# Hybrid decoder block: constant fills moved to VectorE, input buffers moved to the other end of SBUF, small parameter loads and compression weights requested by ScalarE

## The chip, the cores and the metric

The kernel runs on one core of a Trainium2 chip. The metric is the device time of one execution in microseconds (us). The kernel before took 747.08 us, the median of three runs between 744.39 and 748.1 us. A kernel has five engines here: PE (TensorE, matrix products), DVE (VectorE), ACT (ScalarE), POOL (GpSimd) and SP (SyncE), which in this kernel only requests transfers (DMAs).

## What is computed

One layer of a decoder for 512 tokens of width 1024: RMSNorm of `x`, one wide input projection, three token mixers side by side, their gated merge, an output projection, an embedding added through a gate, and a final RMSNorm. Cut to what the start of the kernel does:

```python
h = _rmsnorm(x, norm_g[i])                  # 512 x 1024
proj = h @ w_in[i]                          # every mixer reads columns of this
nkc, nvc = ...                              # 2 x 128 columns of proj
blk = kv[:, idx] + pe[:, None, :]           # _compress: windows of 32 tokens, step 16
hid = silu(einsum('bnlgd,ldh->bngh', blk, w1))
k_cmp, v_cmp = einsum('bngh,hd->bngd', hid, w2)
r, k, v, wl, al = split(xs + (prev - xs) * mu)   # RWKV-7 mixer, columns of proj
```

## The kernel before

Everything that PE multiplies is split into a high part in a short float format and the rest ("high" and "low"), so each product is three matmuls. Weights of the projections come in pieces of 512 columns per partition: SP requests a piece `wr` (L76), ACT rounds it to its high part `wh` (L78), and VectorE or GpSimd forms the rest `wl` (L79). There are four buffers `wr`, so a fifth piece is requested when the first `wl` is done. Two pieces make one block of 128 output columns.

The start of the program goes as follows. GpSimd fills and masks small constant tiles (`trib`, `cmask`, `smask`, `hind`, `hm` and others). SP requests the four 512 KB tiles of `x` into `xs_`, then the first four pieces `wr`, then 14 small transfers of parameters into the tile `prow` (L267: ten parameter vectors and four pieces of `cmp_pe`). For each tile t of `x`, in this order: ACT squares it and sums the squares (`sqj`, L214), VectorE finishes the mean (`rsx`, L215), GpSimd takes the power -0.5 (L216), VectorE scales the tile (L217), PE transposes it in two halves (`xt_ps`, L222), VectorE multiplies each half by the norm's gain (`tg`, L224), ACT rounds it to `hH` (L225, eight of them, kept in the list `hcp`), and GpSimd (first half) or VectorE (second half) forms `hL` (L226).

Then come the two projections `kc` and `vc` that the compression needs, each in two halves of 256 tokens: four groups of 24 matmuls, each evacuated from PSUM by four ACT copies into `kc2` (L264, L265), which stand behind the last `hH` by a written order (`issue_after(hcp[-1])`). PSUM has two buffers `mm_ps` for such groups. After them PE begins block 12 of the RWKV columns (24 matmuls 128x512, then block 4 and so on). Between them stands the compression: 64 small matmuls `hid` that need `w1t`, the compression's weights (L291, four transfers of 512 KB), and `blk`, which is `kc2` plus `pe`. `w2t` (L286, four transfers of 32 KB) is needed later.

The order on each engine is not written by hand. A scheduler at build time orders the instructions, and each engine runs its own list in that order. It also gives each requested transfer one of eight counters, DMAHW0 to DMAHW7, in turn over all queues. A request waits until the transfer that had its counter before has landed.

SBUF pools are stacked from two ends. Pools without a side start at the left; a pool opened after another one has closed takes the same addresses, and its first writers wait for the last readers of the old one. The pool `xp` holds the tiles of `x` and all of `sqj` and `tg`; the pool `cpp`, opened later on the left, holds `kc2`, `w2t`, `w1t` and `blk`.

Of the kernel before, what the change touches and what calls it, by code (L numbers as in the profile page):

```python
# [45 lines left out]
def hybrid_kernel(ctx, tc, x, p, norm_g, w_in, cmp_w1, cmp_w2, cmp_pe, sg_ln_g, sg_ln_b, sg_w, sg_b,  # L46
# [3 lines left out]
    V, S, G, PE, SY = nc.vector, nc.scalar, nc.gpsimd, nc.tensor, nc.sync  # L50
# [45 lines left out]
    identb = const.tile([128, 128], BF, name="identb")  # L96
    V.tensor_copy(identb, ident)
    trib = const.tile([128, 128], BF, name="trib")
    G.memset(trib, 0.0)
    G.affine_select(out=trib, in_=trib, pattern=[[-1, 128]], compare_op=OP.is_ge, fill=NEG, base=0,  # L100
                    channel_multiplier=1)
    cmask = const.tile([128, 4, 32], BF, name="cmask")
    G.memset(cmask, 0.0)
    G.affine_select(out=cmask, in_=cmask, pattern=[[128, 4], [-16, 32]], compare_op=OP.is_ge, fill=NEG,
                    base=-31, channel_multiplier=1)
    rowm = const.tile([128, 1], F32, name="rowm")
    G.memset(rowm, 1.0)
    G.affine_select(out=rowm, in_=rowm, pattern=[[0, 1]], compare_op=OP.is_ge, fill=0.0, base=-31,
                    channel_multiplier=1)
    gmask = const.tile([128, 2, 64], BF, name="gmask")  # L110
    G.memset(gmask, 1.0)
    for r in (0, 64):
        for ar in range(2):
            G.affine_select(out=gmask[r:r + 64, ar, :], in_=gmask[r:r + 64, ar, :], pattern=[[1, 64]],
                            compare_op=OP.is_ge, fill=0.0, base=ar - 1, channel_multiplier=-1)
    smask = const.tile([128, 8, 64], BF, name="smask")
    G.memset(smask, 1.0)
    G.memset(smask[:, :, 0:1], 0.0)
    tri = const.tile([128, 128], BF, name="tri")
    G.memset(tri, 1.0)  # L120
    G.affine_select(out=tri, in_=tri, pattern=[[1, 128]], compare_op=OP.is_ge, fill=0.0, base=0,
                    channel_multiplier=-1)
    mhalf = const.tile([128, 32], F32, name="mhalf")
    G.memset(mhalf, -0.5)
    bones = const.tile([128, 128], BF, name="bones")
    G.memset(bones, 0.0)
    G.memset(bones[0:64, 0:64], 1.0)
    G.memset(bones[64:128, 64:128], 1.0)
    hind = const.tile([128, 4, 8], F32, name="hind")
    G.memset(hind, 0.0)  # L130
    for q in range(4):
        for e in range(2):
            G.memset(hind[e * 64:e * 64 + 64, q, 2 * q + e:2 * q + e + 1], 1.0)

    ng8 = const.tile([8, 128], F32, name="ng8")
    ngp = const.tile([128, 8], F32, name="ngp")
# [4 lines left out]
    def pc(nm, i=0, n=1):  # L141
        return par[:, pcol[nm] + i:pcol[nm] + i + n]
# [28 lines left out]


    hcp = []
    xp_ctx = ExitStack()
    xp = xp_ctx.enter_context(tc.tile_pool(name="xp", bufs=1))
    xps = xp_ctx.enter_context(tc.tile_pool(name="xps", bufs=XP, space=PSUM))
    xs_ = xp.tile([128, 4, 1024], F32, name="xs_")
    ssx = xp.tile([128, 4], F32, name="ssx")
# [1 line left out]
    S.dma_start(ng8, norm_g[0].rearrange("(a b) -> a b", b=128))  # L180
    for t in range(4):
        SY.dma_start(xs_[:, t, :], x[t * 128:(t + 1) * 128, :])
    pw_ctx = ExitStack()
    pw = pw_ctx.enter_context(tc.tile_pool(name="pw", bufs=1, side="right"))
    prow = pw.tile([128, 128], F32, name="prow")
    G.memset(prow, 0.0)
    row = 0
    pls = []
    for nm, src in (("mu", rk_mu), ("w0", rk_w0), ("a0", rk_a0),
# [11 lines left out]
                        cmp_pe[0, kv, lh * 16:lh * 16 + 16, :]))  # L201
    row += 32
    assert row <= 128

    dr = {}
    for nm, w in (("su", 512), ("sv", 512), ("sz", 512), ("rz", 512), ("nz", 512), ("y1", 512), ("sg", 512)):
# [31 lines left out]
    kcst = const.tile([128, 2, 2, 32], R, name="kcst")  # L238
    vcst = const.tile([128, 2, 128], R, name="vcst")
    hm = const.tile([128, 4], F32, name="hm")  # L240
    G.memset(hm, 0.0)
    for hh in range(4):
        G.memset(hm[32 * hh:32 * hh + 32, hh:hh + 1], 1.0)
    cp_ctx = ExitStack()
    cpp = cp_ctx.enter_context(tc.tile_pool(name="cpp", bufs=1))
    cps = cp_ctx.enter_context(tc.tile_pool(name="cps", bufs=1, space=PSUM))
# [5 lines left out]
    for half in range(2):  # L252
        c0 = half * 256
        for kv in range(2):
# [7 lines left out]
            with tc.issue_after(hcp[-1]):  # L262
                for g in range(2):
                    S.copy(kc2[0:64, kv, g, c0:c0 + 256], ps[g * 64:g * 64 + 64, :256])  # L264
                    S.copy(kc2[64:128, kv, g, c0 - sh:c0 + 240], ps[g * 64:g * 64 + 64, 16 - sh:256])  # L265
    for o, i in pls:
        SY.dma_start(o, i)  # L267
    pp_ps = cps.tile([128, 128], F32, tag="par", name="par_ps")
    PE.transpose(pp_ps, prow, ident)
    V.tensor_copy(par, pp_ps)  # L270
# [12 lines left out]
    w2t = cpp.tile([128, 2, 128], F32, name="w2t")  # L283
    for kv in range(2):
        for d in range(2):
            SY.dma_start(w2t[:, kv, d * 64:d * 64 + 64], cmp_w2[0, kv])  # L286
    w1, bl = [], []
    for kv in range(2):
        w1t = cpp.tile([128, 16, 128], F32, tag="w1t", name="w1t", bufs=2)
        for lh in range(2):  # L290
            SY.dma_start(w1t[lh * 64:lh * 64 + 64], cmp_w1[0, kv, lh * 16:lh * 16 + 16].rearrange("l d h -> d l h"))  # L291
        blk = cpp.tile([128, 16, 64], F32, tag="blk", name="blk", bufs=2)
        src = kc2[:, kv].rearrange("p g (n l) -> p l (g n)", l=16)
        V.tensor_tensor(blk, src, pc("pe", kv * 16, 16).unsqueeze(2).to_broadcast([128, 16, 64]), OP.add)
        w1.append(w1t)
        bl.append(blk)
# [68 lines left out]
    for i, src in ((0, rk_w2), (1, rk_a2)):  # L365
        a, o = (slice(0, 64), slice(64, 128)) if i == 0 else (slice(64, 128), slice(0, 64))
# [447 lines left out]
    for i in ATT:  # L814
# [21 lines left out]
        for g in range(2):  # L836
# [13 lines left out]
            for b in range(2):  # L850
# [3 lines left out]
                for hh in range(4):  # L854
                    h = g * 4 + hh
# [167 lines left out]
```

## Time and profile before

| | us |
|---|---|
| median of 3 runs | 747.08 (744.39 to 748.1) |
| the profiled execution, its own time | 744.63 |
| its span in the profile | 742.8 |
| PE busy in the span | 714.5 (96%) |
| ScalarE, VectorE, GpSimd busy | 353.8, 408.6, 287.0 |

The span is what the profile covers, from the first to the last instruction; 1.8 us of the execution lie around it. PE is busy almost throughout, so a delay matters where PE stands still, and a gain elsewhere matters only if it lets PE start sooner.

### The profile page before, as it was taken

To read this page: it belongs to the slowest core of one execution; us is meant where nothing else is said; L and a number is where in the kernel's file an instruction comes from. 1 tells how busy PE (TensorE), PEld (TensorE's weight loads), DVE (VectorE), ACT (ScalarE), POOL (GpSimd) and SP (SyncE) were. 2 spreads that over 40 slices of the span, in tenths; PEclk is the share of its full clock that TensorE was granted. 3 is DMA by queue.
4 is the path that set the end of the run, shared out by engine and by line. 5 is a ranking of instruction groups with operands and counts; after the bars stand their busy time and mean duration, and the time that the engine had idled before them with its cause. 6 is when DMAs were issued, how large, how long until landed. Compare 5 with 4: busy or idle time off the path is not lost.

```text
span 742.8 us, 13074 instructions
## 1 busy us (share of the span) xinstructions
PE 714.5 (96%) x4941; PEld 606.7 (82%) x4941; DVE 408.6 (55%) x776; ACT 353.8 (48%) x743; POOL 287.0 (39%) x275
## 2 busy tenths in 40 slices
PE   4999999999999999989999999989999999999995
PEld 4888788999878987779877778867877888998995
DVE  6531587758843863565676565397555223226345
ACT  6554555542363342335565554576554333227453
POOL 6444640120220263300144345333445565356563
PEclk9999999999999999999999999999999999999999
DMA  5853122125536364427433212201228334132212
GB/s 194 188 140 100 48 81 71 41 85 146 156 105 224 101 184 117 116 86 232 124 97 103 58 43 71 71 16 42 53 62 268 96 91 127 59 114 72 80 63 114
DMA packets 106689, 78.73 MB, mean 106 GB/s; under 512 B 5569, under 2 KB 97282, under 8 KB 106626
## 3 DMA queue, kind: packets, MB, share of 16 engines
q1 hardware_dynamic: 105890, 75.27, 35.5%
q10 hardware_dynamic: 736, 2.63, 0.9%
q8 instruction: 39, 0.64, 0.4%
q14 instruction: 24, 0.20, 0.1%
HBM read 67.91 MB, written 9.96 MB: 105 GB/s over the span
## 4 chain that ended last, share of the span: by engine, by line
PE 88%; DVE 4%; ACT 2%; DMA 2%; issue 1%; POOL 1%; SPq 1%; ACTq 0%; POOLq 0%; DVEq 0%
PE mm_ps L62 70%; PE s_ps L62 3%; PE o_ps L62 2%; PE g_ps L62 2%; PE p_ps L875 2%; DMA w1t<-in_cmp_w_dram 1%; PE Yp L62 1%; DVE mx L861 1%; PE u_ps L62 1%; ACT wh L78 1%; PE xt_ps L222 1%; PE r_ps L62 1%; PE mx_ps L62 1%; DVE pl L879 1%; PE bk_ps L477 1%
## 5 line engine op out<-in xcount | busy, mean ns | idle before, releaser
L79 POOL TENSOR_TENSOR wl<-wr,wh 128x512 fp32r<-128x512 f32 x144 | 192.6, 1346 | 278.9 <-ACT wh L78 257.6
L78 ACT CAST wh<-wr 128x512 fp32r<-128x512 f32 (+1 forms) x194 | 119.4, 620 | 166.5 <-PE mm_ps L62 114.9
L62 PE MATMUL mm_ps<-hH,wh 128*128 128x512 f32 (+1 forms) x440 | 174.9, 398 | 3.3 <-ACT wh L78 1.9
L62 PE MATMUL mm_ps<-hL,wh 128*128 128x512 f32 (+1 forms) x440 | 171.6, 390 | 0.0
L62 PE MATMUL mm_ps<-hH,wl 128*128 128x512 f32 (+1 forms) x440 | 171.1, 389 | 0.0
L62 PEld LDWEIGHTS mm_ps<-hH,wh 128*128 128x128 f32 x440 | 83.5, 190 | 20.7 <-ACT wh L78 2.2
L62 PEld LDWEIGHTS mm_ps<-hH,wl 128*128 128x128 f32 x440 | 83.2, 189 | 17.4 <-issue 0.2
L62 PEld LDWEIGHTS mm_ps<-hL,wh 128*128 128x128 f32 x440 | 83.6, 190 | 16.5 <-issue 0.2
L62 PE MATMUL mm_ps<-wh,hL 128*128 128x256 f32 (+1 forms) x224 | 65.0, 291 | 0.0
L62 PE MATMUL mm_ps<-wh,hH 128*128 128x256 f32 (+1 forms) x224 | 63.8, 286 | 0.0
L62 PE MATMUL mm_ps<-wl,hH 128*128 128x256 f32 (+1 forms) x224 | 63.7, 285 | 0.0
L79 DVE TENSOR_TENSOR wl<-wr,wh 128x512 fp32r<-128x512 f32 (+1 forms) x50 | 38.0, 768 | 26.8 <-ACT wh L78 26.7
L62 PEld LDWEIGHTS mm_ps<-wh,hL 128*128 128x128 f32 x224 | 42.2, 188 | 1.1 <-issue 0.5
L62 PEld LDWEIGHTS mm_ps<-wh,hH 128*128 128x128 f32 x224 | 42.1, 188 | 1.2 <-issue 0.5
L62 PEld LDWEIGHTS mm_ps<-wl,hH 128*128 128x128 f32 x224 | 42.2, 188 | 0.5
L879 DVE TENSOR_TENSOR pl<-p_ps,ph 128x512 fp32r<-128x512 f32 x40 | 27.1, 685 | 25.7 <-ACT ph L878 25.6
L62 PE MATMUL mm_ps<-ysH,wh 128*128 128x512 f32 x96 | 38.6, 402 | 0.1
L62 PE MATMUL mm_ps<-ysL,wh 128*128 128x512 f32 x96 | 38.4, 400 | 0.2 <-DVE ysL L725 0.2
L62 PE MATMUL mm_ps<-ysH,wl 128*128 128x512 f32 x96 | 38.2, 398 | 0.0
L862 ACT ACTIVATE P<-s_ps,mx 128x512 f32<-128x512 f32 (+3 forms) x64 | 33.4, 531 | 7.9 <-DVE mx L861 5.5
L62 PE MATMUL mm_ps<-wh,mH 128*128 128x256 f32 x128 | 35.9, 286 | 0.0
L62 PE MATMUL mm_ps<-wl,hT 128*128 128x256 f32 x128 | 35.8, 281 | 0.0
(337 smaller groups left out, 1434.6 us busy)
## 6 DMA issues: line engine op xcount, KB each, us to landing
wr<-in_w_in_dram SPq DMA_DIRECT2D x130, 256.0 KB
wr<-in_w_branch_dram SPq DMA_DIRECT2D x24, 256.0 KB
wr<-in_w_o_dram SPq DMA_DIRECT2D x16, 256.0 KB
wr<-in_w_ple_gate_dram SPq DMA_DIRECT2D x16, 256.0 KB
xs__129<-in_x_dram SPq DMA_DIRECT2D x4, 512.0 KB
w1t<-in_cmp_w_dram SPq DMA_DIRECT2D x4, 512.0 KB
x<-in_x_dram ACTq DMA_DIRECT2D x4, 512.0 KB
out_dram<-x SPq DMA_DIRECT2D x8, 256.0 KB
```

What stands on the lines that cost most here:

```text
L62: return PE.matmul(o, a, b, start=start, stop=stop, **kw).ins
L78: S.copy(h[:, :m], raw[:, :m])
L79: ph_["l"].tensor_tensor(l[:, :m], raw[:, :m], f(h[:, :m]), OP.subtract)
L222: PE.transpose(ps[:, k, :], xs_[:, t, (4 * a + k) * 128:(4 * a + k + 1) * 128], ident)
L477: PE.transpose(ps[:, c - c0, :], bk[:, c, 0:2].rearrange("p s t -> p (s t)"), ident)
L861: V.tensor_reduce(mx[:, hh:hh + 1], s_ps[:, :W], axis=AX.X, op=OP.max, negate=True)
L862: S.activation(P[:, hh, :W], s_ps[:, :W], AF.Exp, bias=mx[:, hh:hh + 1], accum_out=sm[:, hh:hh + 1])
L875: PE.transpose(p_ps[:, hh * 128:hh * 128 + 128], P[:, hh, kt * 128:kt * 128 + 128], ident)
L879: V.tensor_tensor(pl, p_ps, f(ph), OP.subtract)
```

## The change

It has four parts. Most fills of constant tiles go from GpSimd to VectorE, and so does the fill of `prow`; the masks themselves (`affine_select`) stay on GpSimd. The pools `pw` and `xp` are opened on the right, so `xp` no longer shares addresses with `cpp`. The 14 parameter loads into `prow` are requested by ScalarE (`S.dma_start`), in the code just behind the requests for `x`. The eight requests for `w2t` and `w1t` go from SP to ScalarE, each behind the last `hH` (`hcp[-1]`).

```diff
-    G.memset(trib, 0.0)
+    V.memset(trib, 0.0)
     G.affine_select(out=trib, in_=trib, pattern=[[-1, 128]], compare_op=OP.is_ge, fill=NEG, base=0,
                     channel_multiplier=1)
...
-    G.memset(hind, 0.0)
+    V.memset(hind, 0.0)
     for q in range(4):
         for e in range(2):
-            G.memset(hind[e * 64:e * 64 + 64, q, 2 * q + e:2 * q + e + 1], 1.0)
+            V.memset(hind[e * 64:e * 64 + 64, q, 2 * q + e:2 * q + e + 1], 1.0)
...
     hcp = []
+    pw_ctx = ExitStack()
+    pw = pw_ctx.enter_context(tc.tile_pool(name="pw", bufs=1, side="right"))
     xp_ctx = ExitStack()
-    xp = xp_ctx.enter_context(tc.tile_pool(name="xp", bufs=1))
+    xp = xp_ctx.enter_context(tc.tile_pool(name="xp", bufs=1, side="right"))
...
     for t in range(4):
         SY.dma_start(xs_[:, t, :], x[t * 128:(t + 1) * 128, :])
-    pw_ctx = ExitStack()
-    pw = pw_ctx.enter_context(tc.tile_pool(name="pw", bufs=1, side="right"))
     prow = pw.tile([128, 128], F32, name="prow")
-    G.memset(prow, 0.0)
+    V.memset(prow, 0.0)
...
     assert row <= 128
+    for o, i in pls:
+        S.dma_start(o, i)
...
-    for o, i in pls:
-        SY.dma_start(o, i)
     pp_ps = cps.tile([128, 128], F32, tag="par", name="par_ps")
...
     for kv in range(2):
         for d in range(2):
-            SY.dma_start(w2t[:, kv, d * 64:d * 64 + 64], cmp_w2[0, kv])
+            with tc.issue_after(hcp[-1]):
+                S.dma_start(w2t[:, kv, d * 64:d * 64 + 64], cmp_w2[0, kv])
...
         for lh in range(2):
-            SY.dma_start(w1t[lh * 64:lh * 64 + 64], cmp_w1[0, kv, lh * 16:lh * 16 + 16].rearrange("l d h -> d l h"))
+            with tc.issue_after(hcp[-1]):
+                S.dma_start(w1t[lh * 64:lh * 64 + 64],
+                            cmp_w1[0, kv, lh * 16:lh * 16 + 16].rearrange("l d h -> d l h"))
```

The built programs show where the requests came to stand. First ScalarE's list at the start of the program, before (all of its first rows up to the first rounding of `x`):

```order
L180 DMA ng_115<-in_norm_g_dram 8x128
L214 ACT_TABLE_LOAD
L214 ACTIVATE sqj,ssx<-xs__129 128x1024 [waits DMAHW1_49]
L214 ACTIVATE sqj,ssx<-xs__129 128x1024 [waits DMAHW2_49]
L214 ACTIVATE sqj,ssx<-xs__129 128x1024 [waits DMAHW3_49,Activation_49]
L214 ACTIVATE sqj,ssx<-xs__129 128x1024 [waits DMAHW4_49,Activation_49]
L225 CAST hH<-tg 128x4x128 [waits DVE_49] x4
```

And in the changed program, from the eighth row of the list; ahead of these stand the requests for `norm_g` and six of the parameters:

```order
L205 DMA prow<-in_rk_lnx_g_dram 4x128 [waits DMAHW7_49]
L205 DMA prow<-in_rk_lnx_b_dram 4x128 [waits DMAHW0_49]
L205 DMA prow<-in_ple_norm_g_dram 8x128 [waits DMAHW1_49]
L205 DMA prow<-in_sg_b_dram 8x128 [waits DMAHW2_49]
L205 DMA prow<-in_cmp_pe_dram 16x64 [waits DMAHW3_49]
L205 DMA prow<-in_cmp_pe_dram 16x64 [waits DMAHW4_49]
L205 DMA prow<-in_cmp_pe_dram 16x64 [waits DMAHW5_49]
L205 DMA prow<-in_cmp_pe_dram 16x64 [waits DMAHW6_49]
L216 ACT_TABLE_LOAD
L216 ACTIVATE sqj,ssx<-xs__132 128x1024 x2
L216 ACTIVATE sqj,ssx<-xs__132 128x1024 [waits Activation_49] x2
```

All 14 requests moved ahead of the table load and of the first square, and the squares have no wait of their own on a transfer any more.

SP's list at the start, before:

```order
L182 DMA xs__129<-in_x_dram 128x1024 x4
L76 DMA wr<-in_w_in_dram 128x4x128 x3
L76 DMA wr<-in_w_in_dram 128x4x128 [waits DMAHW0_49]
L267 DMA prow<-in_rk_mu_dram 13x128 [waits DMAHW1_49,Pool_49]
L267 DMA prow<-in_rk_w_dram 4x128 [waits DMAHW2_49]
```

And in the changed program, from the same place:

```order
L184 DMA xs__132<-in_x_dram 128x1024 x4
L76 DMA wr<-in_w_in_dram 128x4x128
L76 DMA wr<-in_w_in_dram 128x4x128 [waits DMAHW1_49]
L76 DMA wr<-in_w_in_dram 128x4x128 [waits DMAHW3_49]
L76 DMA wr<-in_w_in_dram 128x4x128 [waits DMAHW5_49]
L76 DMA wr<-in_w_in_dram 128x4x128 [waits DMAHW7_49,DVE_49]
```

The parameters are gone from SP's list. With 14 transfers now taking counters in between, the four tiles of `x` have DMAHW1, 2, 3 and 5, and the first four pieces `wr` have DMAHW7, 1, 3 and 5. So the second, third and fourth piece wait for the first, third and fourth tile of `x`; and on ScalarE `lnx_g` waits for the first piece, `ple_norm_g` for the second, the first part of `cmp_pe` for the third and its third part for the fourth.

The third place is ScalarE's list behind the last `hH`, before:

```order
L225 CAST hH<-tg 128x4x128 [waits DVE_49]
L264 COPY kc_267<-mm_ps 64x256 [waits DVE_49,PE_49,Pool_49]
L265 COPY kc_267<-mm_ps 64x240
L264 COPY kc_267<-mm_ps 64x256
L265 COPY kc_267<-mm_ps 64x240
L264 COPY kc_267<-mm_ps 64x256 [waits PE_49]
L265 COPY kc_267<-mm_ps 64x240
L264 COPY kc_267<-mm_ps 64x256
L265 COPY kc_267<-mm_ps 64x240
L78 CAST wh<-wr 128x512 [waits DMAHW4_49,PE_49]
L78 CAST wh<-wr 128x512 [waits DMAHW5_49,PE_49]
```

And in the changed program, behind the last `hH` and the first two copies:

```order
L266 COPY kc_281<-mm_ps 64x256
L267 COPY kc_281<-mm_ps 64x240
L287 DMA w2t<-in_cmp_w_dram 128x64 [waits DMAHW3_49]
L287 DMA w2t<-in_cmp_w_dram 128x64 [waits DMAHW4_49]
L287 DMA w2t<-in_cmp_w_dram 128x64 [waits DMAHW5_49]
L287 DMA w2t<-in_cmp_w_dram 128x64
L266 COPY kc_281<-mm_ps 64x256 [waits PE_49]
L267 COPY kc_281<-mm_ps 64x240
L266 COPY kc_281<-mm_ps 64x256
L267 COPY kc_281<-mm_ps 64x240
L293 DMA w1t<-in_cmp_w_dram 64x16x128 [waits DMAHW1_49]
L293 DMA w1t<-in_cmp_w_dram 64x16x128 [waits DMAHW3_49]
```

Two more `w1t` requests stand behind the third group of four copies, and the roundings `wh` of the next pieces come behind the fourth group. The first copy no longer waits for VectorE's `hL`. Further down, PE's list has the same matmuls in nearly the same order.

## Rows read from the trace of the kernel before

**Rows 1.** The page: span, and busy time and share of each engine.

```profile
span 742.8 us, 13074 instructions
PE 714.5 (96%) x4941; PEld 606.7 (82%) x4941; DVE 408.6 (55%) x776; ACT 353.8 (48%) x743; POOL 287.0 (39%) x275
```

**Rows 2.** Who PE waited for, 0 to 50 us: total, times, longest.

```profile
PE xt_ps L222 <- DVE rsx L215: 5.0, 1, 5.0
...
PE mm_ps L62 <- ACT kc L265: 1.4, 1, 1.4
PE hid L62 <- DMA w1t<-in_cmp_w_dram: 0.2, 1, 0.2
```

**Rows 3.** The same, 50 us to the end (first and last of 11 rows).

```profile
PE o_ps L62 <- DVE pl L847: 2.1, 2, 1.2
...
PE mm_ps L62 <- DVE ysL L725: 0.2, 1, 0.2
```

**Rows 4.** ACT's timeline: start, duration, engine, line, instruction, idle before and releaser.

```profile
1.41 1.28 ACT L214 ACT_TABLE_LOAD   x1 [1.41 <-PEq L1011]
4.63 1.06 ACT L214 ACTIVATE sqj<-xs__129 128x1024 f32<-128x1024 f32 x1 [1.93 <-DMA xs__129<-in_x_dram]
...
5.86 1.06 ACT L214 ACTIVATE sqj<-xs__129 128x1024 f32<-128x1024 f32 x1
...
9.52 1.06 ACT L214 ACTIVATE sqj<-xs__129 128x1024 f32<-128x1024 f32 x1 [0.16 <-DMA xs__129<-in_x_dram]
```

**Rows 5.** SP's timeline of requests, 12 to 32 us: start, time to issue.

```profile
12.58 0.25 SPq L267 DMA_DIRECT2D prow<-in_rk_lnx_b_dram  x1
...
13.55 1.70 SPq L267 DMA_DIRECT2D prow<-in_cmp_pe_dram  x4
...
17.86 3.92 SPq L76 DMA_DIRECT2D wr<-in_w_in_dram  x4
23.85 2.17 SPq L286 DMA_DIRECT2D w2t<-in_cmp_w_dram  x4
26.06 5.54 SPq L291 DMA_DIRECT2D w1t<-in_cmp_w_dram  x4
```

**Rows 6.** DVE's timeline, 5 to 24 us.

```profile
5.81 0.15 DVE L215 TENSOR_SCALAR rsx<-ssx 128x1 f32<-128x1 f32 x1 [2.23 <-ACT sqj L214]
...
9.02 0.76 DVE L217 TENSOR_SCALAR xs__129<-xs__129,rsx 128x1024 f32<-128x1024 f32 x1 [0.67 <-POOL rsx L216]
9.69 0.15 DVE L215 TENSOR_SCALAR rsx<-ssx 128x1 f32<-128x1 f32 x1
...
16.70 1.28 DVE L79 TENSOR_TENSOR wl<-wr,wh 128x512 fp32r<-128x512 f32 x2
...
21.30 2.39 DVE L226 TENSOR_TENSOR hL<-tg,hH 128x512 fp32r<-128x512 f32 x2
```

**Rows 7.** POOL's timeline, 6 to 30 us.

```profile
6.94 0.56 POOL L216 TENSOR_TENSOR rsx<-rsx,mhalf 128x1 f32<-128x1 f32 x1
...
27.69 2.68 POOL L79 TENSOR_TENSOR wl<-wr,wh 128x512 fp32r<-128x512 f32 x2 [3.36 <-ACT wh L78]
```

**Rows 8.** ACT's timeline, 20 to 26 us.

```profile
20.95 0.62 ACT L78 CAST wh<-wr 128x512 fp32r<-128x512 f32 x1 [1.71 <-DMA wr<-in_w_in_dram]
21.48 0.61 ACT L225 CAST hH<-tg 128x512 fp32r<-128x512 f32 x1
23.80 0.37 ACT L264 COPY kc<-mm_ps 64x256 f32<-64x256 f32 x1 [1.71 <-DVE hL L226]
...
25.30 0.37 ACT L264 COPY kc<-mm_ps 64x256 f32<-64x256 f32 x1
```

**Rows 9.** The chain that ended last, 28 to 48 us: start, duration, what.

```profile
28.91 9.80 DMA w1t<-in_cmp_w_dram
...
38.84 3.68 PE hid L62 x62
42.52 5.31 PE mm_ps L62 x22
```

More of the change, by code (lines that the diff above doesn't have):

```diff
@@ L102, in hybrid_kernel @@
     cmask = const.tile([128, 4, 32], BF, name="cmask")
-    G.memset(cmask, 0.0)
+    V.memset(cmask, 0.0)
     G.affine_select(out=cmask, in_=cmask, pattern=[[128, 4], [-16, 32]], compare_op=OP.is_ge, fill=NEG,
@@ L106, in hybrid_kernel @@
     rowm = const.tile([128, 1], F32, name="rowm")
-    G.memset(rowm, 1.0)
+    V.memset(rowm, 1.0)
     G.affine_select(out=rowm, in_=rowm, pattern=[[0, 1]], compare_op=OP.is_ge, fill=0.0, base=-31,
@@ L110, in hybrid_kernel @@
     gmask = const.tile([128, 2, 64], BF, name="gmask")
-    G.memset(gmask, 1.0)
+    V.memset(gmask, 1.0)
     for r in (0, 64):
@@ L116, in hybrid_kernel @@
     smask = const.tile([128, 8, 64], BF, name="smask")
-    G.memset(smask, 1.0)
-    G.memset(smask[:, :, 0:1], 0.0)
+    V.memset(smask, 1.0)
+    V.memset(smask[:, :, 0:1], 0.0)
     tri = const.tile([128, 128], BF, name="tri")
-    G.memset(tri, 1.0)
+    V.memset(tri, 1.0)
     G.affine_select(out=tri, in_=tri, pattern=[[1, 128]], compare_op=OP.is_ge, fill=0.0, base=0,
@@ L125, in hybrid_kernel @@
     bones = const.tile([128, 128], BF, name="bones")
-    G.memset(bones, 0.0)
-    G.memset(bones[0:64, 0:64], 1.0)
-    G.memset(bones[64:128, 64:128], 1.0)
+    V.memset(bones, 0.0)
+    V.memset(bones[0:64, 0:64], 1.0)
+    V.memset(bones[64:128, 64:128], 1.0)
     hind = const.tile([128, 4, 8], F32, name="hind")
-    G.memset(hind, 0.0)
+    V.memset(hind, 0.0)
     for q in range(4):
         for e in range(2):
-            G.memset(hind[e * 64:e * 64 + 64, q, 2 * q + e:2 * q + e + 1], 1.0)
+            V.memset(hind[e * 64:e * 64 + 64, q, 2 * q + e:2 * q + e + 1], 1.0)
     ng8 = const.tile([8, 128], F32, name="ng8")
@@ L240, in hybrid_kernel @@
     hm = const.tile([128, 4], F32, name="hm")
-    G.memset(hm, 0.0)
+    V.memset(hm, 0.0)
     for hh in range(4):
-        G.memset(hm[32 * hh:32 * hh + 32, hh:hh + 1], 1.0)
+        V.memset(hm[32 * hh:32 * hh + 32, hh:hh + 1], 1.0)
     cp_ctx = ExitStack()
```

## The prediction

> **What bounds the kernel now.** I read the page first: PE is busy for 714.5 of 742.8 us [rows 1], so PE's list sets the time and only its idle 28.3 us can be gained or added to. Then the waits of PE, in two stretches. Up to 50 us there are few large ones: 5.0 us before the transposes, which wait for the first tile's statistics, 1.4 us for the copies of `kc`, 0.2 us for `w1t` [rows 2]. From 50 us to the end there are eleven small ones between 2.1 and 0.2 us, together 8.6 us [rows 3]; they are waits on VectorE and ScalarE for results that themselves follow from PE's. So what the change does to the start of the kernel goes through to the end almost in full: the list behind 50 us is the same, PE has hardly a gap there to swallow a delay, and nothing there starts sooner than its inputs.
>
> I therefore follow one chain, from the first square on ScalarE to the end of the 64 `hid` matmuls, which in the kernel before is at 38.84 + 3.68 = 42.52 us [rows 9].
>
> **What holds the first square.** Before, the table load is done at 1.41 + 1.28 = 2.69 us and the first square starts at 4.63 us, when the first tile has landed; the second at 5.86, the last at 9.52 us, again with a tile's landing [rows 4]. In the changed list 14 requests stand ahead of the table load. An engine's list is in order, as SP's timeline shows for such requests: `lnx_b` was issued at 12.58 us [rows 5] because it shared its counter with the fourth `wr`, so that row also dates the landing of the fourth piece. Now the third part of `cmp_pe` waits for the fourth `wr` on ScalarE, and that piece is requested only when the last tile of `x` has landed.
>
> When does that piece land? By one way: last tile at 9.5 us [rows 4], plus the time from the request of a `wr` to its rounding, 20.95 - 17.86 = 3.09 us [rows 5, 8]: 12.6 us. By the other: the same 3 MB must come in as before, when the fourth piece had landed at 12.58 us. Both say 12.6. Bound below: the tiles could land closer together if fewer `wr` run beside them; the first two squares are 1.23 us apart without a wait, so a last tile at 4.63 + 3 x 1.23 = 8.3 us is conceivable, 1.2 us sooner. Behind it follow two requests of 1.70 / 4 = 0.43 us [rows 5], the table load of 1.28 us [rows 4] and gaps of some 0.1 us between them: 12.6 + 0.86 + 1.28 + 0.1 = 14.8 us. **The first square starts at S = 14.8 us instead of 4.63, 10.2 us later.** The other waits of these requests lie earlier: transfers of the small parameters, `x` and the first three pieces.
>
> The table load's price has a second answer. The Trainium skill ("ScalarE: Activation LUTs", What ACT_TABLE_LOAD costs) gives about 1283 ns for the load and another 1380 ns of drain for a switch of the set. The trace agrees on the load with its 1.28 us; whether a drain follows it cannot show, since the first square waited 1.93 us for its tile anyway [rows 4]. By the page the sum below would be 1.4 us larger; it goes by the row.
>
> **From S to the last `hH`.** Now all of `x` is in SBUF, so nothing waits for tiles any more and VectorE's list decides. In its new order two statistics stand before the second scaling, so it waits for the third square: 1.18 us from a square to its `rsx` (5.81 - 4.63) [rows 4, 6] and two squares of 1.23 give S + 3.64. From there its list runs on, priced start to start: three scalings of 0.67 (9.02 to 9.69), nine instructions 128x512 (six `tg`, two `hL`, the first `wl`) of 0.60 to 0.68 (1.28 for two) and two `rsx` of some 0.08: 2.0 + 5.5 + 0.1 = 7.6 us [rows 6]. The first `wl` is done at S + 11.3. That frees the first `wr` buffer; the fifth piece takes 3.09 us to arrive [rows 5, 8], its `wh` and the last `hH` 20.95 to 22.09 = 1.14 us [rows 8]. **The last `hH` is done at T = S + 15.5 = 30.3 us, before at 22.09: 8.2 us later.** Of the 10.2 us two are won back because squares and scalings no longer wait for tiles. Not less than about 7.0 (the tiles sooner); not more than 9.3, since a pair `hL` beside GpSimd's work took 2.39 instead of 1.28 us [rows 6], 1.1 us more.
>
> **The parts that gain.** Fills off GpSimd: its first power started at 6.94 [rows 7], 1.1 us after the statistic at 5.81, because the fills were still running. That wait is gone, but it lies ahead of S and no longer counts. The fills cost VectorE nothing: it idled 2.23 us before its first `rsx` [rows 6], and now has until S. Addresses: the first copy of `kc` waited 1.71 us for `hL` because `kc2` lay where `tg` had been [rows 8]; now it may start at T. SP's time for the parameters, up to 13.55 + 1.70 = 15.25 us [rows 5], is free now, but what comes next in its list, the fifth piece, needs the first `wl` anyway.
>
> Here a rule speaks against the change. The Trainium skill ("DMA: Bandwidth & Descriptors", Issuing engines are not separate DMA queues) says that requests from several engines share the same 16 engines and save only the time to initiate them. No row shows a second queue at work in this stretch. By the page no transfer lands sooner for its new queue, and the sum counts none that does; the other way would at most bring `prow` sooner, for which nobody waits.
>
> **From T to the end of `hid`.** Before: 42.52 - 22.09 = 20.4 us, in which PE also did 29 matmuls 128x512. After, ScalarE's list: four copies 1.50 (23.80 to 25.30) [rows 8], the four `w2t` 2.17 [rows 5], four copies, two `w1t`, four copies, two `w1t`, four copies, the next `wh` 0.62 [rows 8], then GpSimd's `wl` 2.68 / 2 = 1.34 [rows 7]. Nothing in this list is reordered around a request, so PE waits behind it: for the second PSUM buffer, then for the sixth piece. The `w1t` requests are the open price: 5.54 us for four [rows 5], in a row whose later requests were held up by the earlier ones. At that price 6.00 + 2.17 + 5.54 + 0.62 + 1.34 = 15.7 us; then ten matmuls of 5.31 / 22 = 0.24 and the `hid` of 3.68 [rows 9] give 15.7 + 2.4 + 3.7 = 21.8, and by then PE has done 26 of the 29 large matmuls, so 0.7 more: 22.5 us, or 2.1 more than before. Below: if a `w1t` took no longer to issue than a `w2t` (0.54), 3.4 us less, -1.3. Above: the last `w1t` took 9.80 us from the start of its request to its landing [rows 9]; issued at about T + 10, that is T + 19.8, and with `hid` and 0.7 the end is T + 24.2, 3.8 more. I take +1.0: issue is spread between copies, which holds the requests up less, and the transfers have less beside them.
>
> **Sum.** 8.2 + 1.0 = 9.2 us later at the end of `hid`, and so at the end. The profiled execution, 744.63 us, becomes 753.8; the median of the runs shown is 2.45 us above that execution and would become 756.3. I say 755.0, between the two.
>
> **The rivals.** *The delay is absorbed (no change).* If the later engines run ahead of PE, the small waits behind 50 us shrink. They are 8.6 us in all [rows 3]. If all went, 9.2 - 8.6 = 0.6 would remain: 745 to 748 us. Against it: they wait for results made from PE's own, which come as late. It decides only if at least 5.5 us go. Chance 0.07. *The start gets shorter (faster).* If the requests pass without holding ScalarE, so that the first square still starts at 4.63 us, GpSimd's 1.1 us and the 1.4 us that PE waited for `kc` [rows 2] fall away, and with the 0.5 us of SP's queue ahead of the fifth piece 3.0 us, 741.6 to 744.1 us. It decides if the first square starts before about 7 us. Against it: the counters of the order above. Chance 0.04, half of it by over 0.5%. *The second half dominates (slower still).* If ScalarE pays 2.69 us for each late `w1t` as well as the drain, or `w1t` lands as late as the upper end says, the end comes 8.2 + 3.8 = 12 us later or more: 757 to 760 us. Chance 0.14. *The small delay.* Tiles sooner, cheap requests: 7.0 - 1.3 = 5.7 us, 750.3 to 752.8 us. Chance 0.15. The forecast, 752 to 757.5 us, has the remaining 0.60.
>
> **The numbers.** A measurement of this kernel cannot tell less than about 0.5%, 3.7 us, from no change. Slower by more than that: forecast, small and large delay, 0.89, less 0.02 for a small delay that stays below the bound: 0.87. Same: 0.07 + 0.02 + 0.02 = 0.11. Faster: 0.02. The range reaches from the small delay to the large one, 750.5 to 760.
>
> **What would show it.** ScalarE's first square near 14.8 us, with the requests of `prow` ahead of it and waits in between; the last `hH` near 30.3; the first copy of `kc` right behind it; `hid` ending near 52; all that follows shifted alike. It would be wrong if squares stand at 5 to 7 us, if the fourth `wr` lands well before 12 us, or if PE's waits behind 50 us get shorter by several us.

## The result

The changed kernel took 759.11 us, the median of six runs between 757.77 and 760.22, against 747.07 us before, the median of six runs between 744.39 and 748.1 us. The medians are 12.0 us apart. The ratio estimated from the single runs is 1.0175, with a 95% interval of 1.0161 to 1.0189, and stands for 13.1 us; where this text says that the change costs 13.1 us, it means this ratio. The direction was as predicted. The size was not: 755.0 us was forecast, with a range of 750.5 to 760.0. The median of 759.11 us lies inside that range, but 1.0175 times the 747.08 us shown before the change is 760.15 us, just past its end.

### The profile page after: what moved, and what is told of

It reads as the page before. It is cut to its first block, busy times and chain, and to the rows that moved or that the text cites. A ratio compares the mean times of both kernels' runs of the same rounds, so it can differ in the third digit from the quotient of the medians.

```text
span 758.5 us, 13070 instructions
## 1 busy us (share of the span) xinstructions
PE 717.8 (95%) x4941; PEld 608.8 (80%) x4941; DVE 410.9 (54%) x801; ACT 353.0 (47%) x743; POOL 283.2 (37%) x250
## 4 chain that ended last, share of the span: by engine, by line
PE 87%; DVE 4%; DMA 4%; ACT 2%; issue 1%; POOL 0%; ACTq 0%; SPq 0%; POOLq 0%; DVEq 0%
PE mm_ps L62 69%; PE s_ps L62 3%; PE o_ps L62 2%; PE g_ps L62 2%; PE p_ps L878 2%; DMA w1t<-in_cmp_w_dram 2%; PE Yp L62 1%; DMA wr<-in_w_in_dram 1%; DMA xs__132<-in_x_dram 1%; PE u_ps L62 1%; DVE mx L864 1%; PE xt_ps L224 1%; PE hid L62 1%; PE r_ps L62 1%; PE mx_ps L62 1%
```

## The profile after

The page of the changed kernel, its span and its busy times, beside [rows 1]:

```profile
span 758.5 us, 13070 instructions
PE 717.8 (95%) x4941; PEld 608.8 (80%) x4941; DVE 410.9 (54%) x801; ACT 353.0 (47%) x743; POOL 283.2 (37%) x250
```

PE is hardly busier than before; what came is idle time. ScalarE's timeline at the start, beside [rows 4] (start, duration, queue or engine, line, instruction, idle before and releaser):

```profile
2.18 0.35 ACTq L205 DMA_DIRECT2D prow<-in_rk_mu_dram  x1
...
5.62 0.26 ACTq L205 DMA_DIRECT2D prow<-in_rk_kk_dram  x1
...
10.05 0.25 ACTq L205 DMA_DIRECT2D prow<-in_rk_lnx_g_dram  x1
...
11.55 1.74 ACTq L205 DMA_DIRECT2D prow<-in_cmp_pe_dram  x4
13.32 1.28 ACT L216 ACT_TABLE_LOAD   x1 [13.32 <-DMA prow<-in_cmp_pe_dram]
14.62 1.06 ACT L216 ACTIVATE sqj<-xs__132 128x1024 f32<-128x1024 f32 x1
```

The 14 requests each take a quarter to half a microsecond, but stretch over 11 us, because most wait for an older transfer. The table load comes behind them and the first square at 14.62 us, 10 us later than before. The load ends at 13.32 + 1.28 = 14.60 and the square starts 0.02 us later. Ahead of the load there is no gap either: the last request ends at 11.55 + 1.74 = 13.29. So the drain of about 1380 ns that the Trainium skill ("ScalarE: Activation LUTs", What ACT_TABLE_LOAD costs) adds to the load for a switch of the set is not seen at this load, the first of the program; the measurement decides, and the sum went by the row rightly.

ScalarE's timeline from the last `hH` on, beside [rows 8]:

```profile
30.32 0.62 ACT L78 CAST wh<-wr 128x512 fp32r<-128x512 f32 x1 [0.72 <-DMA wr<-in_w_in_dram]
...
30.85 0.62 ACT L227 CAST hH<-tg 128x512 fp32r<-128x512 f32 x1
...
31.38 0.36 ACT L266 COPY kc<-mm_ps 64x256 f32<-64x256 f32 x1
...
32.73 0.70 ACTq L293 DMA_DIRECT2D w1t<-in_cmp_w_dram  x1
32.87 0.36 ACT L266 COPY kc<-mm_ps 64x256 f32<-64x256 f32 x1
33.24 0.35 ACT L267 COPY kc<-mm_ps 64x240 f32<-64x240 f32 x1
33.47 0.68 ACTq L293 DMA_DIRECT2D w1t<-in_cmp_w_dram  x1
33.60 0.37 ACT L266 COPY kc<-mm_ps 64x256 f32<-64x256 f32 x1
...
36.05 0.36 ACT L266 COPY kc<-mm_ps 64x256 f32<-64x256 f32 x1 [1.71 <-PE mm_ps L62]
```

Two things are to be seen. The first copy of `kc` follows the last `hH` at once. And a request of 0.68 us at 33.47 stands between copies that follow each other without a gap (33.24 + 0.35 = 33.59, the next at 33.60): this request had nothing left to wait for, ran beside ScalarE's work and held nothing up. The copies later waited for PE, not for requests.

Who PE waited for, 0 to 60 us, beside [rows 2], and then the chain that ended last, beside [rows 9]:

```profile
PE xt_ps L224 <- DVE rsx L217: 14.1, 1, 14.1
PE hid L62 <- DMA w1t<-in_cmp_w_dram: 3.7, 2, 3.5
```

```profile
36.73 13.09 DMA w1t<-in_cmp_w_dram
49.83 0.14 issue
49.96 5.04 PE hid L62 x62
55.00 6.21 PE mm_ps L62 x26
```

The wait for the first statistics went from 5.0 to 14.1 us. A second one, 0.2 us before, is now large: the last `w1t` landed 13.09 us after its request, PE stood still for 3.5 us, and then the same 62 small matmuls took 5.04 instead of 3.68 us. The windows (length; busy time and count of PE, PEld, DVE, ACT and POOL; granted clock; DMA share; GB/s) show why:

```profile
48.00:50.00 2.00, 0.04 (x2) 0.07 (x3) 0.00 (x0) 0.00 (x0) 0.00 (x0) 0.84 1.20 270
50.00:52.00 2.00, 2.00 (x20) 2.00 (x22) 0.05 (x1) 1.46 (x3) 0.79 (x1) 0.50 0.74 203
52.00:54.00 2.00, 2.00 (x34) 2.00 (x32) 0.80 (x2) 1.62 (x4) 1.74 (x2) 0.81 0.16 27
54.00:56.00 2.00, 2.00 (x23) 1.65 (x19) 1.94 (x4) 1.80 (x4) 0.00 (x0) 1.00 0.87 224
...
60.00:200.00 140.00, 140.00 (x926) 120.97 (x925) 87.22 (x142) 67.77 (x136) 41.88 (x37) 1.00 0.30 83
```

PE did almost nothing from 48 to 50 us; from 50 to 52 the granted clock is 0.50, which is 1.2 of the 2.4 GHz. Set against each other matmul by matmul, PE is 9.1 us late at the first transpose, 13.2 us at 60 us, and stays so to 217 us: PE is busy for all 140 us between 60 and 200, and nothing is won back. The profiled spans differ by 15.7 us, 2.5 more. Of these 3.9 come between 217 and 345 us, where the granted clock of this execution falls to 0.50 in two short stretches (230.3 to 233.6 and 336.1 to 342.8 us), and 1.5 go again between 500 and 600 us, where that of the execution before falls (545.2 to 548.4 us). Where such a late stretch falls differs between executions: the profile with only the fills moved, a program as fast as the one before, has two of them near 220 and 325 us. So the text goes by the first 60 us of a trace and by the medians.

## The theories

**Theory A.** The 14 requests in front of the squares are nearly all of it: they hold up the first square by 10 us. Requests behind the last `hH` cost ScalarE nothing. **Theory B.** Requests on ScalarE's list cost its copies, so the second half of the delay is the eight requests for `w2t` and `w1t`. Fills and addresses were counted as small gains by both. A third possibility is that fills or addresses cost the time; the expectations call it rival C, and theory B rival B. Of the runs, each with its own kernel before beside it, the first two decide on A.

## The experiments

**The parameters on SP again.** The changed kernel without its third part:

```diff
-    for o, i in pls:            # ahead of the squares
-        S.dma_start(o, i)
+    for o, i in pls:            # where they stood before
+        SY.dma_start(o, i)
```

> The changed kernel with the 14 parameter requests back on SP behind the first four weight pieces; fills, pools and the w2t and w1t requests on ScalarE stay as changed. Theory A (ScalarE's squares stand behind requests that wait for the weight pieces' counters, worth 9.4 us at the last hH; the rest of the 13.2 us comes from w1t landing after that): first square near 4.6 us, last hH at 22 us or a little sooner, 745 to 750 us. Rival B (the requests of w2t and w1t on ScalarE cost most, by holding the engine or by a late landing): first square 4.6 us, but PE late behind the last hH by 5 us or more, 752 us or more. Rival C (fills on VectorE or the pools' new place cost the time): 755 us or more.

748.76 us, ratio 1.0032 (1.0017 to 1.0047): 10 us of the 13 are gone. The first square is at 4.59 and the last `hH` is done at 21.36 us. Set against the kernel before matmul by matmul, PE is then 2.5 us ahead from the second half of `kc` on, of which 1.6 come there, since the copies of `kc` no longer wait. It loses that lead again. Its chain:

```profile
23.67 10.23 DMA w1t<-in_cmp_w_dram
33.89 0.14 issue
34.03 0.66 PE hid L62 x2
...
39.48 3.68 PE hid L62 x62
```

`w1t` is requested behind the last `hH` and lands beside the weight pieces; PE waits 2.5 us for it, does the next large matmuls at a granted clock of 0.50 (fourteen in 4.72 us, where 22 took 5.31 before [rows 9]), and the end of `hid`, 39.48 + 3.68 = 43.16, is 0.6 us later than before, with 26 instead of 22 large matmuls still to come: PE is 1.3 us late from there to 60 us.

**The parameters alone.** The kernel before, with only these requests on ScalarE:

```diff
+    for o, i in pls:            # ahead of the squares
+        S.dma_start(o, i)
...
-    for o, i in pls:
-        SY.dma_start(o, i)
```

> The kernel before with one edit: the 14 parameter requests on ScalarE, where the change puts them; fills on GpSimd, pools and SP's w2t and w1t requests as before. Theory A: first square at 13 to 15 us, time 754 to 758 us. Rival B: within 2 us of before. Rival C: within 2 us of before.

757.45 us, ratio 1.0154 (1.0133 to 1.0174). The table load is at 15.56, the first square at 16.85 us, later than the 13 to 15 us expected, and PE's wait for the first statistics is 16.3 us. Theory A stands: this one part costs 11 us by itself, and 10 within the change.

**The compression's weights alone.** The kernel before, with only the requests for `w2t` and `w1t` on ScalarE:

```diff
-            SY.dma_start(w2t[...], cmp_w2[0, kv])
+            with tc.issue_after(hcp[-1]):
+                S.dma_start(w2t[...], cmp_w2[0, kv])
... (w1t alike)
```

> The kernel before, with only the eight requests for w2t and w1t moved to ScalarE behind the last hH. Theory A (requests run beside ScalarE's compute and only the waits in front of squares hurt): first square at 4.6 us, last hH near 22, w1t requested at 23 to 30 us, landing at 36 to 40, end of hid within 2 us of the 42.5 us of before: 745 to 749. Theory B (requests on ScalarE's list cost its copies): copies of kc 2 to 7 us late and 751 or more.

745.35 us, ratio 0.9988 (0.9978 to 0.9999). Theory B falls: the same eight requests on ScalarE cost nothing when the rest is left as it was: the end of `hid` is 1.1 us later, 43.64, but with more of the large matmuls done ahead of it. The wait for `w1t` is not there either: it is requested from 26.29 us on, and large matmuls fill PE until `hid`.

**Fills and pools.** The changed kernel with all requests back on SP, so only its first two parts:

```diff
-            with tc.issue_after(hcp[-1]):
-                S.dma_start(w2t[...], cmp_w2[0, kv])
+            SY.dma_start(w2t[...], cmp_w2[0, kv])
... (w1t and prow alike)
```

> The changed kernel with all its requests back on SP, so only the fills on VectorE and the pools on the right are left. Theory A: 743 to 747 us, since GpSimd's first power starts about 1 us sooner and the first copy of kc no longer waits 1.7 us for hL; w1t may be requested sooner, as nothing holds its buffer. Rival C: 755 us or more. Rival B says nothing here beyond no loss.

752.71 us, ratio 1.0085 (1.0067 to 1.0102). I had expected a small gain: the parts counted as gains cost 6.4 us. SP's timeline shows an order that [rows 5] does not have:

```profile
16.85 4.71 SPq L291 DMA_DIRECT2D w1t<-in_cmp_w_dram  x4
21.66 5.81 SPq L76 DMA_DIRECT2D wr<-in_w_in_dram  x4
```

Before, `w1t` came behind the fifth weight piece; now ahead of it. So two more runs took these two parts one by one.

**Fills alone.** The kernel before with the fills of the diff on VectorE and nothing else:

```diff
-    G.memset(trib, 0.0)
+    V.memset(trib, 0.0)
... (all fills of the change alike)
```

> The kernel before, with only the fills on VectorE. Theory A: GpSimd's first power starts 1.1 us sooner (at 5.8 instead of 6.94), everything else in place: 745.5 to 747. Rival: VectorE's fills hold its first statistics, or the order of requests on SP changes as it did with the pools moved too: 749 or more.

746.09 us, ratio 1.0001 (0.9988 to 1.0014). GpSimd's first power is at 6.04 instead of 6.94 us, right behind its statistic, and the first transpose is 0.9 us sooner too; the lead is lost again at the copies of `kc`, for which PE waits 2.0 us. At 60 us PE is 1.6 and at 323 us 3.7 us late in this profile, yet the medians are equal: a difference of that size between two profiles is no proof of an effect.

**Pools alone.** The kernel before with `pw` and `xp` on the right:

```diff
-    xp = xp_ctx.enter_context(tc.tile_pool(name="xp", bufs=1))
+    xp = xp_ctx.enter_context(tc.tile_pool(name="xp", bufs=1, side="right"))
```

> The kernel before, with only the pools pw and xp opened on the right. Theory A (the pools, not the fills, cost the 6 us that fills and pools cost together, because w1t's tiles need no longer wait for tiles of x, so SP's list takes their requests ahead of the fifth weight piece): fifth piece lands near 30 us, ScalarE's copies of kc stand behind its rounding, PE waits some 4 us for them: 751 to 754. Rival (fills and pools are both needed, or the fills are it): 745 to 748.

750.36 us, ratio 1.0067 (1.0045 to 1.0090), a little under what theory A said. The pools are it. SP's timeline, ScalarE's timeline, and who PE waited for up to 60 us:

```profile
16.77 4.81 SPq L291 DMA_DIRECT2D w1t<-in_cmp_w_dram  x4
21.69 5.76 SPq L76 DMA_DIRECT2D wr<-in_w_in_dram  x4
```

```profile
30.59 0.62 ACT L78 CAST wh<-wr 128x512 fp32r<-128x512 f32 x1 [5.15 <-DMA wr<-in_w_in_dram]
31.51 0.62 ACT L78 CAST wh<-wr 128x512 fp32r<-128x512 f32 x1 [0.30 <-DMA wr<-in_w_in_dram]
32.16 0.37 ACT L264 COPY kc<-mm_ps 64x256 f32<-64x256 f32 x1
```

```profile
PE mm_ps L62 <- ACT kc L265: 4.1, 1, 4.1
```

`w1t` no longer lies where the tiles of `x` were, its request has nothing to wait for, and the scheduler puts it ahead of the fifth piece. That piece is requested at 21.69 instead of 17.86 us and lands beside 2 MB of `w1t`; its rounding starts at 30.59 instead of 20.95. The copies of `kc` stand behind the roundings on ScalarE, and PE behind the copies. The row names the copy as what PE waited for; the DMA of the roundings ahead of it is the cause. And the wait is only half of the price: set against the kernel before matmul by matmul, PE is 2.6 us late when it resumes at 33.71 and 5.2 us at 40 us, because it resumes at the lower clock:

```profile
30.00:32.00 2.00, 0.00 (x0) 0.00 (x0) 0.00 (x0) 1.11 (x2) 0.71 (x1) 1.00 1.13 319
...
34.00:36.00 2.00, 2.00 (x5) 1.53 (x5) 1.65 (x1) 1.94 (x6) 1.62 (x1) 0.50 0.88 219
36.00:38.00 2.00, 2.00 (x6) 1.60 (x5) 1.62 (x1) 0.96 (x2) 2.00 (x2) 0.50 0.14 36
```

With `w1t` off SP's list this cost goes: from fills and pools (752.71) to those with the weights on ScalarE (748.76) the time falls by 4.0 us. With the squares late it does not appear either, as the next run shows: there `w1t` stands on SP ahead of the fifth piece, but its last request has been made at 16.69 us, the fifth piece is requested at 25.56 us, when the first `wl` is done, and PE waits no more than 0.3 us for the copies of `kc`.

**The weights on SP again.** The changed kernel without its fourth part:

```diff
-            with tc.issue_after(hcp[-1]):
-                S.dma_start(w2t[...], cmp_w2[0, kv])
+            SY.dma_start(w2t[...], cmp_w2[0, kv])
... (w1t alike)
```

> The changed kernel with only the w2t and w1t requests back on SP; the 14 parameter requests stay on ScalarE ahead of the squares, but in this order they share their counters among themselves and with norm_g and the second tile, not with the weight pieces. Theory A: the first square waits only for the requests' own round trips, at 9 to 13 us instead of 14.6, and w1t, requested early, no longer holds PE: 750 to 754 us. If it is the mere number of requests ahead of the squares and not the pieces' counters, the first square stays at 14 us or later. Rival B: 747 us or less.

756.05 us, ratio 1.0127 (1.0108 to 1.0147), more than the 750 to 754 us that theory A said. In this program the parameters take four of the eight counters in turn, and wait for one another, for `norm_g` and for the second tile of `x`, no longer for the weight pieces. I expected the first square at 9 to 13 us; it came at 14.35:

```profile
2.18 0.35 ACTq L205 DMA_DIRECT2D prow<-in_rk_mu_dram  x1
...
5.66 0.25 ACTq L205 DMA_DIRECT2D prow<-in_rk_kk_dram  x1
7.17 0.25 ACTq L205 DMA_DIRECT2D prow<-in_rk_ka_dram  x1
...
9.89 0.26 ACTq L205 DMA_DIRECT2D prow<-in_rk_lnx_b_dram  x1
```

`kk` waits for the second tile of `x`, `ka` for `mu`, which was requested at 2.18 us, and `lnx_b` for `kk`: 5.0 and 4.2 us for 6.5 and 2 KB, while `x` and the weight pieces stream in. So the fourth piece is not what makes the first square late. In the changed kernel the third part of `cmp_pe` did wait for it, but only 0.16 us (it was issued at 12.50, and the request ahead of it ended at 11.91 + 0.43 = 12.34), and without that wait the queue of small transfers, most behind an older one, ends within 0.3 us of the same time. The mere number of requests is not it either: their own issue times add up to 4.6 of the 10.8 us from 2.18 to 13.02, and the rest is waiting. No run gave the requests counters without a wait, so how early the square could come behind them is open. `w1t` lands early here and `hid` has no wait: it ends at 45.96 + 3.71 = 49.67 us. The change, whose only difference is the fourth part, ends it 5.3 us later and takes 3.6 us more by the two ratios: here that part costs time.

**The parameters behind the squares.** The changed kernel, the requests still on ScalarE, held behind the last square:

```diff
-    for o, i in pls:
-        S.dma_start(o, i)
...
+    with tc.issue_after(sq_):      # sq_: the last square
+        for o, i in pls:
+            S.dma_start(o, i)
```

> The changed kernel, but the 14 parameter requests on ScalarE are held behind the last square. Theory A (the requests in front of the squares are what costs): first square at about 4.6 us; the requests now stand among the hH and wait there for older transfers, so hH comes later by 1 to 4 us; 747 to 753. Rival (it is enough that the requests are on ScalarE, wherever they stand): as the changed kernel, 757 to 760.

752.46 us, ratio 1.0079 (1.0058 to 1.0099), as theory A said: half of the loss is gone with the place alone. The first square is at 4.51. What is left stands among the `hH`:

```profile
15.00 0.62 ACT L225 CAST hH<-tg 128x512 fp32r<-128x512 f32 x1 [1.05 <-DMA prow<-in_cmp_pe_dram]
```

A rounding of `x` waits for a small transfer that it does not need, only because a request in front of it on ScalarE does. The rest is the pattern of the pools: `w1t` is requested from 19.14 us on, one weight piece of 256 KB then takes 9.14 us to land, and PE waits 3.8 us for the copies of `kc`.

**w1t sooner, in the changed kernel.** One word of the change:

```diff
-            with tc.issue_after(hcp[-1]):      # the requests of w1t
+            with tc.issue_after(hcp[3]):
```

> The changed kernel, with the four w1t requests behind the fourth hH instead of the last; the parameters stay on ScalarE ahead of the squares. Theory A (of the 13 us, 3.5 are w1t's late landing and 1.4 the low clock in hid behind it): first square still at 14.6 us, w1t lands before hid, hid takes 3.7 us again: 754 to 757. Rival (the engines have no room for w1t any sooner: the fifth piece or the pieces of block 12 land later by as much): 758 to 761.

754.47 us, ratio 1.0115 (1.0091 to 1.0138), as theory A said: 4.5 us less than the change. The first square is at 14.96, as late as in the change. The requests go out between 22.38 and 27.12 us, `w1t` is there before `hid`, PE has no wait for it, and the chain reads:

```profile
48.39 3.64 PE hid L62 x62
```

The 3.5 us of waiting and the 1.4 us of `hid` at the low clock are gone together. The rival is not quite absent: the fifth piece took 8.15 us to land instead of about 3, and PE waited 1.6 us for the copies of `kc`. This is the part of the delay that the prediction had mis-sized.

**Two tries for a better kernel.** First, the kernel with the parameters on SP again and `w1t` requested behind the fourth `hH`:

```diff
-    for o, i in pls:                           # and issued by SP, as before
-        S.dma_start(o, i)
...
-            with tc.issue_after(hcp[-1]):      # the requests of w1t
+            with tc.issue_after(hcp[3]):
```

> The changed kernel with the parameters requested by SP again and the four w1t requests behind the fourth hH instead of the last. Theory A: w1t lands before 30 us, PE no longer waits for it before hid and keeps the 4 us that it was ahead at the second half of kc: 742 to 746. Rival: w1t's transfers share the engines with the fifth piece, which then lands some 5 us later and holds the copies of kc: 750 to 753.

748.13 us, ratio 1.0025 (1.0014 to 1.0036): neither. The lead to be kept was 2.5 us and not the 4 that the expectation names. `hid` had no wait, but ended at 43.36, 0.8 us later than before: the last `hH` was done at 22.17, PE waited 1.0 us for GpSimd's `hL` and 1.0 for a rounding. Second, the kernel before with the weights on ScalarE and `kc2` alone on the right:

```diff
+    kcp = kcp_ctx.enter_context(tc.tile_pool(name="kcp", bufs=1, side="right"))
...
-    kc2 = cpp.tile([128, 2, 2, 512], F32, name="kc2")
+    kc2 = kcp.tile([128, 2, 2, 512], F32, name="kc2")
... (w2t and w1t as in the run with these weights alone)
```

> The kernel before, with w2t and w1t requested by ScalarE behind the last hH, and kc2 alone put on the right, away from the tiles of x. Theory A: the first copy of kc starts right behind the last hH (near 21.5 instead of 23.8 us), PE's 1.4 to 2.3 us before the second half of kc go, and the fifth piece keeps its place: 743 to 744.5. Rival: the time gained there is lost in front of hid, because w1t lands no sooner: 745 to 747.

746.14 us, ratio 0.9996 (0.9983 to 1.0009): the rival. The copies start at 21.82, PE is 2 us ahead at the second half of `kc`, and gives it back before `hid`:

```profile
PE mm_ps L62 <- ACT wh L78: 1.4, 1, 1.4
PE hid L62 <- DMA w1t<-in_cmp_w_dram: 1.0, 1, 1.0
```

So the best kernel here is the one before with the compression's weights on ScalarE, 745.35 us, 0.1% below it, with an interval that just excludes no change; among eleven such intervals that is weak evidence of a gain.

## Why the prediction was wrong

**What bounds the kernel.** Right. PE's list sets the time, the start's delay goes through, and the waits behind 60 us absorbed nothing.

**The first square.** Right in time, 14.8 forecast and 14.62 measured. The reason held only in part, and the exact hit is partly luck: the fourth piece did let the third part of `cmp_pe` go at 12.50 us, as forecast, but the queue of requests ahead of it had itself got there only 0.16 us sooner, which the prediction did not reckon with; with other counters (the weights on SP again) the square comes at 14.35. The bound "tiles sooner" had no effect.

**From the first square to the last `hH`.** Forecast 15.5 us, measured 31.47 - 14.62 = 16.85; the last `hH` came 9.4 us later instead of 8.2. VectorE's instructions were priced at 0.60 to 0.68 us. The first `wl` alone, for which the fifth piece waits, took 1.75 (the three in the row 2.96), and a scaling 1.17:

```profile
23.10 1.17 DVE L219 TENSOR_SCALAR xs__132<-xs__132,rsx 128x1024 f32<-128x1024 f32 x1
...
25.39 2.96 DVE L79 TENSOR_TENSOR wl<-wr,wh 128x512 fp32r<-128x512 f32 x3
```

GpSimd ran `hL` from 22.12 and from 25.32 us, in the same stretches. The prediction named this slowdown, 1.1 us, as its upper bound and left it out. That GpSimd is the cause is read from the overlap; no run took its work away, and overlap alone does not do it: three `tg` from 20.11 us on, beside another `hL` of GpSimd, took 1.88 us together, as priced.

**From T to the end of `hid`: the step that failed.** I took +1.0 us between bounds of -1.3 and +3.8. Measured: from 31.47 to 55.00 is 23.5 us, before 20.4, so +3.1, and four large matmuls more stand behind `hid` (26 instead of 22 up to the next small product), 0.9 us: +4.0, just past the upper bound. Two things in the step were wrong. It built a list of ScalarE in which the requests cost 7.7 us; they cost its copies nothing. And the last `w1t` was taken to land sooner than by its row because the transfers "have less beside them"; it took 13.09 us instead of 9.80 [rows 9]. What each queue moved in these two stretches (packets, MB, the time that the packets took as a share of the 16 engines' time, which passes 100% where they overlap), first the changed kernel, 36.73 to 49.82 us, then before, 28.91 to 38.71 us:

```profile
q10 hardware_dynamic: 3154, 1.59, 69.5%
q1 hardware_dynamic: 1960, 1.29, 51.2%
```

```profile
q1 hardware_dynamic: 4539, 2.28, 123.4%
```

q10 carries what ScalarE requested (4.90 MB in the whole execution, 2.63 before) and q1 what SP did. The engines moved data at nearly the same rate, 220 against 233 GB/s. But before, `w1t` went by SP's one queue, ahead of later pieces; now SP, which requested two parts of `w2r` and four weight pieces in that stretch, moved 1.29 MB beside 1.59 MB of `w1t`. The Trainium skill ("DMA: Bandwidth & Descriptors", Issuing engines are not separate DMA queues) has the rule that bears on this, that requests from different engines run on the same 16 engines and interleave. The trace agrees, with two queues at 69.5% and 51.2% where one had 123.4%. The prediction used the rule for the gains and not for this landing. That the wait and the clock behind it are the term is shown by `w1t` requested sooner: 4.5 us less, with `hid` back at 3.64 us. That the term ends so near its upper bound is partly luck: the bound had the last request at T + 10 and its landing at T + 19.8; it was made at T + 5.3 and landed at T + 18.4, and the 1.4 us between went again in `hid` at the lower clock, which the prediction had not priced. What came about is nearest to its rival of a dominant second half, 757 to 760 us, which had a chance of 0.14.

**The parts that gain.** Fills: right, nothing. Addresses: the first copy did start at the last `hH`. But that pools also decide when a request may stand in SP's list was not seen; in the whole change it does not show. Alone against the kernel before the parts cost 0 (fills), 4.5 (pools), -0.9 (weights) and 11.1 us (parameters), by medians, 14.7 in all, where the medians of the change are 12.0 apart, a difference that the intervals of these ratios together allow. What shows that the parts do not add is the fourth one: -0.9 us alone, -4.0 us behind fills and pools, and 3.6 us more in the whole change.

**The sum.** 9.4 + 4.0 = 13.4 us against 9.2 forecast; the trace shows 13.2 at 60 us, the ratio stands for 13.1 and the medians are 12.0 apart. Two terms were mis-sized, each a little past the same end of its own bounds. And the forecast of 755.0 us took another 1.3 us off by lying between the profiled execution and the median: added to the median, the sum itself says 756.3.

## What to carry to other kernels

In these runs a DMA request in ScalarE's list was free while it had nothing to wait for, and held up all that stood behind it when it shared a counter with a transfer in flight; put such requests behind the work, not in front of it or among it. A wait on an old address can be useful: it held 2 MB of transfers behind the piece that PE needed first, and taking it away cost 4.5 us. When a load moves, price its landing by the stretch into which it moves, with what the other queues move there, and ask what PE does until then: an idle PE can pay twice, for the wait and for the clock behind it.

## What was not expected of the hardware

Small transfers were slow while large ones streamed: about 5.0 and 4.2 us from request to landing for 6.5 and 2 KB (the weights on SP again). And a short idle stretch of PE can cost twice. Three runs show a granted clock of 0.50 right behind one: 3.5 us before `hid` here, 4.1 us with the pools alone, and 2.5 us with the parameters on SP again, where the windows read:

```profile
32.00:34.00 2.00, 0.00 (x0) 0.00 (x1) 1.01 (x1) 1.26 (x3) 2.00 (x1) 1.00 1.20 220
34.00:36.00 2.00, 1.97 (x5) 1.45 (x6) 0.00 (x0) 0.00 (x0) 2.00 (x3) 0.50 1.23 233
```

What it cost was 1.4 us (`hid`), 2.6 us (5.2 less 2.6) and about 1.3 us (4.72 less 14 x 5.31 / 22), beside the waits themselves. It does not follow every such stretch: with the weights alone PE stood still for 2.3 us before the copies of `kc` were done, and the granted clock stayed at 1.00.
